# Norm outputs finished later: a two-block layer stack with hand-ordered vector work on one core

## The chip, the cores and the metric

One core of one Trainium2 chip runs the whole program. The metric is the device time of one execution in microseconds (us); smaller is better. The kernel before is given with three runs: 951.21, 951.55 and 951.58 us, median 951.55.

## What is computed

The input is 256 tokens of 1,024 channels. A first block (a mixer of three branches, then a gated feed-forward layer, both with RMS norms) is followed by two layers of a second block. The part of the second block that the change touches is, in the reference:

```python
for l in range(DEPTH_2):
    ...
    x = layer_norm(DEEPNORM_ALPHA * x + g1[:, None, :] * y, ln1_g[l], ln1_b[l])
    h = modulate(x, sh2, sc2)
    y = swiglu(h, ffn_w_gate[l], ffn_w_up[l], ffn_w_down[l])
    x = layer_norm(DEEPNORM_ALPHA * x + g2[:, None, :] * y, ln2_g[l], ln2_b[l])
```

`y` is a short convolution in layer 0 and forgetting attention (16 heads) in layer 1. `swiglu(h)` is `(silu(h @ w_gate) * (h @ w_up)) @ w_down` with 2,816 hidden channels. The six modulation vectors come from one vector `c`: `silu(c) @ w_ada + b_ada`.

## The kernel before

Activations lie with 128 channels on the partitions and the 256 tokens along the row, so a 1,024-channel activation is eight tiles (k = 0 to 7). Weights are float32 blocks of 128x128, read eight at a time (512 KB) by DMAs issued on SyncE. Each group of eight is split by ScalarE into a rounded high part `wh` (L145) and by VectorE into the rest `wl` (L151). Activations are split in the same way (`hilo`, L267 and L268). A product is three matmuls: `wh` by high, `wl` by high, `wh` by low. There are five buffers for split groups, and eight PSUM banks: four `acc`, two `lg`, two `ms`.

`single` and `pair` form one or two output columns over all k. `kouter` and `ksteps` take k in the outer loop for several columns, so that a product can begin when tile k = 0 is there. `gemv` forms one of 112 rows of the modulation vectors: a 512 KB DMA and one VectorE instruction (L372). How many of them go beside each unit of product is `grate`, set from the tuple `GR` as each stage begins; `fill` issues them. From any one constant or edit the order on an engine is found by a scheduler with a simulated timeline; `after(a, b)` adds an order to that (a behind b, no semaphore).

A norm ahead of a product is handled in two ways. After the first block's products (`post_rms`), the statistics are formed by matmuls against `rdim`, the reciprocal root by a chain of tiny VectorE instructions (`rsqrt`), and the result is spread by matmuls (`bcast`, L309). `warm` puts idle matmuls into the gaps. In the second block, three of the norms (`deep_norm` with `so`, then `ln_rows`) have a product that begins ahead of the norm: `lazy` multiplies six columns with the tiles that aren't normalised yet; `lazy_outs` then forms `out * R + nm * c0 + c1` from each of the six sums. `ln_next` meanwhile normalises and modulates the eight tiles for the remaining columns: per tile two VectorE instructions (L1071, L1072), two on ScalarE (L944, L267) and the low part on VectorE (L268). In a feed-forward layer the six outputs are three gate and up pairs, and `evac` applies silu, multiplies and splits them. In the attention layer they are six of the eight key tiles.

`unbroken(ins, free, act, head)` says which splits of later weights may go ahead of a norm's chain on VectorE: `free` of them ahead, the others behind the instructions `ins`; `head`, the chain's first instruction, goes behind those that are free. It also puts the next `gemv` behind the last of `ins`. `later` is a list of steps put off; `drain` issues one of them after each pair of columns.

In the attention loop TensorE's order is written by hand: the logits of head pair i, the transposes of pair i - 1, one k-step of the output projection's first four columns (`partial`), the values of pair i - 1.

Lines that the steps below speak of: `evac` L905, the loop over `first` L927, `deep_norm` L957, the freeing multiplication L1058, the addition L1066, the first norm's `rms_cols` L1102, the convolution's tiles L1189, the attention loop L1309 and the end of it L1322.

Of the kernel before, what the change touches and what calls it, by code (L numbers as in the profile page):

```python
# [17 lines left out]
P = 128  # L18
D = 1024
T = 256  # L20
# [9 lines left out]
GR = (0.75, 1.2, 0.375, 0.9, 1.05, 1.4, 0.25)  # L30
# [7 lines left out]
EXP_LN = 6  # L38
WARM = (3, 3, 5, 0)
# [26 lines left out]
class Net:  # L66
# [287 lines left out]
    def accum(self, acc, i, src, eps=0.0):  # L354

        if i == 0:
            self.nc.vector.tensor_scalar(acc, src, eps * NK, None, ALU.add)
        else:
            self.nc.vector.tensor_tensor(acc, acc, src, ALU.add)
# [539 lines left out]
    def ffn(self, l, X, R=None, first=(), rows=None):  # L899
# [3 lines left out]
        MH, ML = [], []  # L903

        def evac(g, u):  # L905
# [16 lines left out]
            MH.append(h)  # L922
            ML.append(lo)
# [33 lines left out]
    def deep_norm(self, wname, X, nk, gcol, ax, so=None, pre=()):  # L957
# [4 lines left out]
        zs, Z = [], ([], [])  # L962
# [5 lines left out]
        for c in range(NK):  # L968
# [11 lines left out]
            if so is not None:  # L980
# [4 lines left out]
                V.scalar_tensor_tensor(l, z, so[:, c, 0:1], h.bitcast(F32), op0=ALU.mult, op1=ALU.subtract)  # L985
# [65 lines left out]
    def lazy_outs(self, pss, R, nm, outs):  # L1051
# [3 lines left out]
        for ps, out in zip(pss, outs):  # L1055
            c = self.tmp("lz_c", (P, 2), bufs=4)
# [21 lines left out]
    def run(self):  # L1078
# [23 lines left out]
        rc = self.rms_cols()  # L1102
        rp = self.bcast(rc)
# [84 lines left out]
        for k in range(NK):  # L1188
            t = x1[k]  # L1189
            i0 = V.tensor_tensor(fg[k], fg[k], rp, ALU.mult)  # L1190
            i1 = V.tensor_tensor(t, t, fg[k], ALU.add)
            h, l = self.modulate(t, sc1[:, k:k + 1], sh1[:, k:k + 1])
# [4 lines left out]
        self.grate = GR[2]  # L1197
        self.pipeline(steps)
        self.unbroken([x[-1] for x in steps[1:]], 2, head=head)
# [57 lines left out]
        ks = []  # L1257
        for o in (0, 4):
            outs = [self.tmp("f_k", bufs=NK) for _ in first[o:o + 4]]
            self.lazy_outs(first[o:o + 4], *rows, outs)  # L1260
# [11 lines left out]
        for k in range(NK):  # L1272
# [5 lines left out]
            XQ[1].append(l)  # L1278
        self.inplace = True
# [25 lines left out]
        with self.tc.manual_schedule(engines={nc.tensor.engine}):  # L1305
# [16 lines left out]
            step(Y, NK - 1)  # L1322
        self.inplace = False
# [162 lines left out]
```

## Time and profile before

| | us |
|---|---|
| median of three runs | 951.55 |
| the profiled execution, its own time | 952.66 |
| its span in the trace | 950.8 |
| TensorE busy with matmuls | 916.2 |
| VectorE busy | 765.5 |
| ScalarE busy | 529.7 |
| SyncE's DMA queue, share of the 16 engines' span | 67.3% |

The profile was taken in one execution. Its span is what the trace covers, and 1.8 us of its time lie around it. An instruction's line is that of the kernel's code; `out<-in` are the program's tile names. Busy time of TensorE is modelled for the ends of matmuls, so it shows gaps in the stream, and not how fast the stream runs. A row's last bracket is the engine's idle time just before the instruction and what ended it.

### The profile page before, as it was taken

To read this page: it belongs to the slowest core of one execution; us is meant where nothing else is said; L and a number is where in the kernel's file an instruction comes from. 1 tells how busy PE (TensorE), PEld (TensorE's weight loads), DVE (VectorE), ACT (ScalarE), POOL (GpSimd) and SP (SyncE) were. 2 spreads that over 40 slices of the span, in tenths; PEclk is the share of its full clock that TensorE was granted. 3 is DMA by queue.
4 is the path that set the end of the run, shared out by engine and by line. 5 is a ranking of instruction groups with operands and counts; after the bars stand their busy time and mean duration, and the time that the engine had idled before them with its cause. 6 is when DMAs were issued, how large, how long until landed. Compare 5 with 4: busy or idle time off the path is not lost.

```text
span 950.8 us, 18969 instructions
## 1 busy us (share of the span) xinstructions
PE 916.2 (96%) x7434; PEld 884.6 (93%) x7434; DVE 765.5 (81%) x1463; ACT 529.7 (56%) x958; POOL 19.9 (2%) x66
## 2 busy tenths in 40 slices
PE   7999999999999899998999999999998999999995
PEld 7888899999999899998999999988887899999995
DVE  7897667999989789679899989898776897665554
ACT  7585755544444465557755454468665486544432
POOL 1111000000000000000000000000000000000001
PEclk9999999999999999999999999999999999999998
DMA  8774337899999787554899999845563458766631
GB/s 297 238 224 136 97 108 266 289 349 326 329 306 394 240 274 262 176 155 133 268 374 351 364 327 342 301 155 159 177 217 114 126 165 271 217 190 186 186 102 45
DMA packets 62345, 219.56 MB, mean 231 GB/s; under 512 B 7112, under 2 KB 8784, under 8 KB 62256
## 3 DMA queue, kind: packets, MB, share of 16 engines
q1 hardware_dynamic: 61056, 215.06, 67.3%
q0 software_dynamic: 1056, 3.16, 1.2%
q8 instruction: 58, 0.95, 0.4%
q14 instruction: 31, 0.25, 0.1%
q10 hardware_dynamic: 144, 0.13, 0.0%
HBM read 217.26 MB, written 2.63 MB: 231 GB/s over the span
## 4 chain that ended last, share of the span: by engine, by line
PE 84%; DVE 8%; ACT 3%; issue 2%; DMA 2%; SPq 0%; DVEq 0%; ACTq 0%
PE acc L165 19%; PE acc L163 19%; PE acc L164 19%; PE acc L198 4%; PE acc L199 4%; PE acc L204 4%; DVE wl L151 3%; PE lg L165 1%; PE lg L163 1%; PE lg L164 1%; DMA raw<-wts 1%; PE acc L254 1%; PE acc L252 1%; PE acc L253 1%; ACT wh L145 1%
## 5 line engine op out<-in xcount | busy, mean ns | idle before, releaser
L145 ACT ACTIVATE wh<-raw 128x1024 fp32r<-128x1024 f32 (+2 forms) x296 | 307.4, 1046 | 230.1 <-PE acc L165 112.4
L151 DVE TENSOR_TENSOR wl<-raw,wh 128x1024 fp32r<-128x1024 f32 (+2 forms) x296 | 355.1, 1208 | 82.8 <-ACT wh L145 80.9
L163 PE MATMUL acc<-yh,wh 128*128 128x256 f32 x544 | 152.3, 280 | 0.9 <-ACT yh L267 0.9
L165 PE MATMUL acc<-yl,wh 128*128 128x256 f32 x544 | 152.6, 281 | 0.5 <-DVE yl L268 0.5
L164 PE MATMUL acc<-yh,wl 128*128 128x256 f32 x544 | 151.9, 280 | 0.0
L163 PE MATMUL acc<-xh,wh 128*128 128x256 f32 x528 | 148.7, 282 | 0.0
L165 PE MATMUL acc<-xl,wh 128*128 128x256 f32 x528 | 148.3, 281 | 0.0
L164 PE MATMUL acc<-mh,wl 128*128 128x256 f32 x528 | 148.2, 281 | 0.0
L165 PE MATMUL acc<-ml,wh 128*128 128x256 f32 x528 | 148.1, 281 | 0.0
L163 PE MATMUL acc<-mh,wh 128*128 128x256 f32 x528 | 148.1, 281 | 0.0
L164 PE MATMUL acc<-xh,wl 128*128 128x256 f32 x528 | 148.0, 280 | 0.0
L372 DVE SCALAR_TENSOR_TENSOR gw<-gw,cact 128x1024 f32<-128x1024 f32 x112 | 135.2, 1220 | 0.6 <-DMA gw<-ada 0.5
L163 PEld LDWEIGHTS acc<-yh,wh 128*128 128x128 f32 x544 | 102.4, 188 | 1.1 <-ACT yh L267 1.1
L165 PEld LDWEIGHTS acc<-yl,wh 128*128 128x128 f32 x544 | 102.1, 188 | 0.8 <-DVE yl L268 0.7
L164 PEld LDWEIGHTS acc<-yh,wl 128*128 128x128 f32 x544 | 102.5, 188 | 0.0
L163 PEld LDWEIGHTS acc<-xh,wh 128*128 128x128 f32 x528 | 99.4, 188 | 1.4 <-issue 0.9
L164 PEld LDWEIGHTS acc<-xh,wl 128*128 128x128 f32 x528 | 99.5, 189 | 0.3
L165 PEld LDWEIGHTS acc<-ml,wh 128*128 128x128 f32 x528 | 99.5, 189 | 0.0
L163 PEld LDWEIGHTS acc<-mh,wh 128*128 128x128 f32 x528 | 99.5, 188 | 0.0
L165 PEld LDWEIGHTS acc<-xl,wh 128*128 128x128 f32 x528 | 99.3, 188 | 0.2 <-issue 0.2
L164 PEld LDWEIGHTS acc<-mh,wl 128*128 128x128 f32 x528 | 99.3, 188 | 0.0
L198 PE MATMUL acc<-xh,wh 128*128 128x256 f32 (+1 forms) x256 | 66.6, 290 | 9.7 <-ACT wh L145 5.5
(416 smaller groups left out, 1635.7 us busy)
## 6 DMA issues: line engine op xcount, KB each, us to landing
raw<-wts SPq DMA_DIRECT2D x288, 512.0 KB, 4.6
gw<-ada SPq DMA_DIRECT2D x112, 512.0 KB, 5.3
raw<-wts SPq DMA_DIRECT2D x6, 256.0 KB, 5.7
m_scr<-m_row POOLq DMA_DIRECT2D x2, 768.0 KB, 6.7
ax<-xT SPq DMA_DIRECT2D x4, 256.0 KB, 4.8
m_b<-m_scr POOLq DMA_DIRECT2D x8, 128.0 KB, 3.8
out<-fg SPq DMA_DIRECT2D x8, 128.0 KB, 1.8
cst<-cst SPq DMA_DIRECT2D x1, 588.5 KB, 6.7
```

The source lines that it names most:

```text
L145: i = self.aw = nc.scalar.activation(self.wh[:, d], r, AF.Copy)
L151: self.anchor = nc.vector.tensor_tensor(self.wl[:, d], r, self.wh[:, d].bitcast(F32), ALU.subtract)
L163: m = [mm(ps, wh, xh, start=start, stop=False), mm(ps, wl, xh, start=False, stop=False), mm(ps, wh, xl, start=False, stop=stop)]
L164: mm(ps, wl, xh, start=False, stop=False),
L165: mm(ps, wh, xl, start=False, stop=stop)]
L198: m.append(mm(outs[i], wh, X[0][k], start=k == 0 and i % per == 0, stop=False))
L199: m.append(mm(outs[i], wl, X[0][k], start=False, stop=False))
L204: m.append(mm(outs[i], wh, X[1][k], start=False, stop=False))
L252: mm(outs[tt], h, wh, start=k == 0 and (tt == 0 or not one), stop=False)
L253: mm(outs[tt], l, wh, start=False, stop=False)
L254: mm(outs[tt], h, wl, start=False, stop=k == NK - 1 and (tt == 1 or not one))
L372: i = nc.vector.scalar_tensor_tensor(t, t, 1.0, self.cact, op0=ALU.mult, op1=ALU.mult, accum_out=self.ada[:, g:g + 1])
```

## The change

The outputs formed ahead of a norm are now freed by their multiplication alone (L1058). The addition, the gate, the product and the split are returned as closures. In the two feed-forward layers they go to `later` (behind the eight residual steps that are there already), so one finished pair of hidden channels is issued beside each of three later pairs of columns; their sums lie in six tiles `fz` of the layer's pool. In the attention layer the six additions are issued after the query tiles. The small tile `lz_c` has six buffers for four.

Beside that: `GR[1]`, `GR[2]` and `GR[4]` move rows of the modulation vectors between stages. The first norm gets an `unbroken` with seven free splits. The convolution's tile k = 0 takes a shorter way from the norm to its high part, with the residual's own update for that tile at the end. After the attention loop the first later weight split goes behind the last softmax maximum, and all others go behind the last low part of the attention output. In the third such norm, the six accumulations of c = 4 to 6 go behind the last low part. The hidden tiles `mh`, `ml` are 256 wide instead of 258, and a pad of 192 bytes is set aside ahead of them by a `memset` on GpSimd.

```diff
-GR = (0.75, 1.2, 0.375, 0.9, 1.05, 1.4, 0.25)
+GR = (0.75, 0.85, 0.65, 0.9, 1.15, 1.4, 0.25)
+SHIFT = 192
+LATE = 3
+FREE0 = 7
...
+    def shift(self, pool, n):
+
+        self.nc.gpsimd.memset(self.tl(pool, [P, n // 4], "pad", bufs=1), 0.0)
...
-            h = self.tl(self.fp, [P, T + 2], "mh", F32R)[:, 0:T]
-            lo = self.tl(self.fp, [P, T + 2], "ml", F32R)[:, 0:T]
+            h = self.tl(self.fp, [P, T], "mh", F32R)
+            lo = self.tl(self.fp, [P, T], "ml", F32R)
...
-            outs = [self.tmp("ff_g" if q % 2 == 0 else "ff_u") for q in range(o, min(2 * n, o + 4))]
-            self.lazy_outs(first[o:o + 4], *rows, outs)
+            outs = [self.tl(self.fp, [P, T], "fz", bufs=6) for q in range(o, min(2 * n, o + 4))]
+            fins = self.lazy_outs(first[o:o + 4], *rows, outs)
             for j in range(0, len(outs), 2):
-                evac(*outs[j:j + 2])
+                self.later.append(lambda a=(len(MH), outs[j], outs[j + 1], fins[j:j + 2]): finish(*a))
+                MH.append(None)
+                ML.append(None)
...
             if so is not None:
+                if pre and c == NK - 1:
+                    for i in late:
+                        self.after(i, lz)
...
-                    self.accum(zacc, c, z)
-                    self.accum(sacc, c, sq)
+                    i = self.accum(zacc, c, z), self.accum(sacc, c, sq)
+                    if c > LATE:
+                        late += i
...
-        for c, out in zip(cs, outs):
+
+        def finish(c, out):
             w = self.tmp("md_h")
-            self.after(A.activation(w, nm, AF.Identity, scale=c[:, 0:1], bias=c[:, 1:2]), a)
-            self.after(V.tensor_tensor(out, out, w, ALU.add), i)
+            self.after(A.activation(w, nm, AF.Identity, scale=c[:, 0:1], bias=c[:, 1:2]), self.his[-1])
+            self.after(V.tensor_tensor(out, out, w, ALU.add), self.steps[-1][-1])
...
         rc = self.rms_cols()
+        self.unbroken([self.tail], FREE0, head=self.head)
...
+            if k == 0:
+                xs, fs = (self.tl(self.lp, [P, T], "ln_w", bufs=4) for _ in range(2))
+                A.activation(xs, t, AF.Identity, scale=sc1[:, 0:1], bias=sh1[:, 0:1])
+                A.activation(fs, fg[0], AF.Copy, scale=sc1[:, 0:1])
+                i0 = V.tensor_tensor(fs, fs, rp, ALU.mult)
+                i1 = V.tensor_tensor(fs, fs, xs, ALU.add)
+                h, l = self.hilo(fs, "x")
...
+        i = V.tensor_tensor(fg[0], fg[0], R, ALU.mult)
+        self.after(i, self.lo)
+        V.tensor_tensor(x1[0], x1[0], fg[0], ALU.add)
...
             step(Y, NK - 1)
+        self.unbroken([self.mxs, self.lo], 0)
```

## Rows read from the trace of the kernel before

**Rows 1.** Page, part 1: engine, busy us, share of the span, instructions.

```profile
PE 916.2 (96%) x7434; PEld 884.6 (93%) x7434; DVE 765.5 (81%) x1463; ACT 529.7 (56%) x958; POOL 19.9 (2%) x66
```

**Rows 2.** Windows by stage: length, busy us (count) per engine, granted clock, DMA.

```profile
314.00:330.00 16.00, 12.44 (x91) 11.25 (x91) 10.86 (x29) 6.64 (x11) 0.13 (x2) 1.00 0.62 199
436.00:452.00 16.00, 13.50 (x108) 12.69 (x107) 16.00 (x38) 14.84 (x31) 0.00 (x0) 1.00 0.44 133
628.00:642.00 14.00, 12.81 (x81) 10.89 (x80) 13.57 (x30) 12.40 (x25) 0.00 (x0) 1.00 0.54 184
642.00:666.00 24.00, 24.00 (x134) 19.86 (x134) 19.74 (x38) 19.13 (x40) 0.00 (x0) 1.00 0.53 158
717.00:732.00 15.00, 12.18 (x85) 10.03 (x84) 8.94 (x17) 6.76 (x17) 0.00 (x0) 0.89 0.55 176
732.00:750.00 18.00, 15.65 (x123) 14.70 (x121) 15.47 (x33) 9.88 (x19) 0.00 (x0) 1.00 0.41 118
```

**Rows 3.** Timeline of VectorE and TensorE, first norm: start, us, engine, instruction, idle.

```profile
28.50 1.23 DVE L151 TENSOR_TENSOR wl<-raw,wh 128x1024 fp32r<-128x1024 f32 x1 [0.85 <-ACT wh L145]
30.39 1.23 DVE L151 TENSOR_TENSOR wl<-raw,wh 128x1024 fp32r<-128x1024 f32 x1
32.22 0.68 PE L309 MATMUL ms<-ident,nw_y 128*128 128x128 f32 x4 [0.90 <-DVE nw_y L290]
```

**Rows 4.** Timeline around the norm ahead of the convolution, by engine.

```profile
314.73 12.39 SPq L369 DMA_DIRECT2D gw<-ada  x5
...
320.96 1.22 DVE L372 SCALAR_TENSOR_TENSOR gw<-gw,cact 128x1024 f32<-128x1024 f32 x1
323.72 1.22 DVE L372 SCALAR_TENSOR_TENSOR gw<-gw,cact 128x1024 f32<-128x1024 f32 x1
...
325.32 0.60 ACT L944 ACTIVATE ln_w<-ax,adac,adac 128x256 f32<-128x256 f32 x1 [2.84 <-DVE ax L1191]
...
326.42 0.39 PE L198 MATMUL acc<-xh,wh 128*128 128x256 f32 x1 [1.77 <-ACT xh L267]
```

**Rows 5.** TensorE's waits, 436 to 452: total us, times, longest; one freeing multiplication.

```profile
PE acc L199 <- DVE wl L151: 2.0, 3, 0.9
PE acc L198 <- DVE ff_g L1058: 0.5, 1, 0.5
...
436.43 0.42 DVE L1058 TENSOR_TENSOR ff_g<-acc,zacc 128x256 f32<-128x256 f32 x1
```

**Rows 6.** Timeline at the key tiles: two additions, and TensorE's wait.

```profile
629.99 0.76 DVE L1066 TENSOR_TENSOR f_k<-f_k,md_h 128x256 f32<-128x256 f32 x2
...
635.07 0.72 PE L254 MATMUL acc<-wl,yh 128*128 128x512 f32 x2 [1.19 <-DVE wl L151]
```

**Rows 7.** Timeline, end of attention and third such norm; the last row a window.

```profile
716.65 4.63 DVE L151 TENSOR_TENSOR wl<-raw,wh 128x1024 fp32r<-128x1024 f32 x4
...
721.52 0.75 DVE L792 TENSOR_REDUCE a_mx<-lg 128x1 f32<-128x256 f32 x2
...
731.49 0.42 DVE L268 TENSOR_TENSOR yl<-ms,yh 128x256 fp32r<-128x256 f32 x1 [4.83 <-ACT yh L267]
...
748.02 0.42 DVE L978 TENSOR_TENSOR p_sq<-fg 128x256 f32<-128x256 f32 x1
...
744.97 0.39 PE L198 MATMUL acc<-xh,wh 128*128 128x258 f32 x1 [2.24 <-DVE fg L971]
...
726.80:730.20 3.40, 3.40 (x18) 0.52 0.34 133
```

**Rows 8.** Timeline of TensorE, the third norm's first remaining column.

```profile
766.75 0.39 PE L198 MATMUL acc<-yh,wh 128*128 128x256 f32 x1 [1.26 <-DVE ff_u L1058]
```

**Rows 9.** Windows of TensorE alone: gate columns (x tiles), then down-projection (mh, ml).

```profile
180.00:250.00 70.00, 70.00 (x598) 1.00 0.93 331
...
556.00:606.00 50.00, 50.00 (x424) 1.00 0.95 333
```

More of the change, by code (lines that the diff above doesn't have):

```diff
@@ L356, in accum @@
         if i == 0:
-            self.nc.vector.tensor_scalar(acc, src, eps * NK, None, ALU.add)
-        else:
-            self.nc.vector.tensor_tensor(acc, acc, src, ALU.add)
+            return self.nc.vector.tensor_scalar(acc, src, eps * NK, None, ALU.add)
+        return self.nc.vector.tensor_tensor(acc, acc, src, ALU.add)
     def gemv(self, n=1):
@@ L903, in ffn, with evac @@
         MH, ML = [], []
-        def evac(g, u):
+        self.shift(self.fp, SHIFT)
+        def evac(g, u, j=None):
             if R is not None:
@@ L917, in evac, with finish @@
                 V.tensor_tensor(m, s, u, ALU.mult)
-            h = self.tl(self.fp, [P, T + 2], "mh", F32R)[:, 0:T]
-            lo = self.tl(self.fp, [P, T + 2], "ml", F32R)[:, 0:T]
+            h = self.tl(self.fp, [P, T], "mh", F32R)
+            lo = self.tl(self.fp, [P, T], "ml", F32R)
             nc.scalar.activation(h, m, AF.Copy)
             self.gbound = V.tensor_tensor(lo, m, h.bitcast(F32), ALU.subtract)
-            MH.append(h)
-            ML.append(lo)
+            if j is None:
+                MH.append(h)
+                ML.append(lo)
+            else:
+                MH[j], ML[j] = h, lo
+        def finish(j, g, u, fins):
+            for f in fins:
+                f()
+            evac(g, u, j)
         wg, wu = f"g{l}", f"u{l}"
@@ L961, in deep_norm @@
         V = nc.vector
-        zs, Z = [], ([], [])
+        zs, Z, late = [], ([], []), []
         if so is None:
@@ L984, in deep_norm @@
                 nc.scalar.activation(h, z, AF.Copy, scale=so[:, c, 0:1])
-                V.scalar_tensor_tensor(l, z, so[:, c, 0:1], h.bitcast(F32), op0=ALU.mult, op1=ALU.subtract)
+                lz = V.scalar_tensor_tensor(l, z, so[:, c, 0:1], h.bitcast(F32), op0=ALU.mult, op1=ALU.subtract)
                 Z[0].append(hf)
@@ L1055, in lazy_outs @@
         for ps, out in zip(pss, outs):
-            c = self.tmp("lz_c", (P, 2), bufs=4)
+            c = self.tmp("lz_c", (P, 2), bufs=6)
             a = A.activation(c, ps[:, T:], AF.Copy)
@@ L1062, in lazy_outs @@
             cs.append(c)
-        for c, out in zip(cs, outs):
+        def finish(c, out):
             w = self.tmp("md_h")
-            self.after(A.activation(w, nm, AF.Identity, scale=c[:, 0:1], bias=c[:, 1:2]), a)
-            self.after(V.tensor_tensor(out, out, w, ALU.add), i)
+            self.after(A.activation(w, nm, AF.Identity, scale=c[:, 0:1], bias=c[:, 1:2]), self.his[-1])
+            self.after(V.tensor_tensor(out, out, w, ALU.add), self.steps[-1][-1])
+        return [lambda c=c, out=out: finish(c, out) for c, out in zip(cs, outs)]
     def ln_mod(self, z, rows, s1, b1, tag="y", pool=None):
@@ L1189, in run @@
             t = x1[k]
-            i0 = V.tensor_tensor(fg[k], fg[k], rp, ALU.mult)
-            i1 = V.tensor_tensor(t, t, fg[k], ALU.add)
-            h, l = self.modulate(t, sc1[:, k:k + 1], sh1[:, k:k + 1])
+            if k == 0:
[5 more added lines that the diff above has]
+                h, l = self.hilo(fs, "x")
+            else:
+                i0 = V.tensor_tensor(fg[k], fg[k], rp, ALU.mult)
+                i1 = V.tensor_tensor(t, t, fg[k], ALU.add)
+                h, l = self.modulate(t, sc1[:, k:k + 1], sh1[:, k:k + 1])
             steps.append([i0, i1, self.lo])
@@ L1197, in run @@
         self.grate = GR[2]
+        R = self.tl(self.lp, [P, T], "rp", bufs=1)
+        A.activation(R, rp, AF.Copy)
         self.pipeline(steps)
+        i = V.tensor_tensor(fg[0], fg[0], R, ALU.mult)
+        self.after(i, self.lo)
+        V.tensor_tensor(x1[0], x1[0], fg[0], ALU.add)
         self.unbroken([x[-1] for x in steps[1:]], 2, head=head)
@@ L1256, in run @@
         x, XK, rows = self.ln_next(zs, rows, so, (g, b), (0, 4, 1, 3, 5, 7))
-        ks = []
+        ks, fins = [], []
         for o in (0, 4):
             outs = [self.tmp("f_k", bufs=NK) for _ in first[o:o + 4]]
-            self.lazy_outs(first[o:o + 4], *rows, outs)
+            fins += self.lazy_outs(first[o:o + 4], *rows, outs)
             ks += outs
@@ L1278, in run @@
             XQ[1].append(l)
+        for f in fins:
+            f()
         self.inplace = True
```

## The prediction, made before the change was run

> **What bounds the kernel now.** I read the busy times first. TensorE is busy for 916.2 of 950.8 us, VectorE for 765.5 [rows 1]. So TensorE leaves 34.6 us idle in all, and a change that adds no matmul can only win from that, from matmuls that follow each other faster, and from stretches at a lower clock. The windows by stage say where the idle time is: 3.56 us ahead of the convolution, 2.50 in the first norm with outputs formed ahead, 1.19 at the key tiles, 2.82 and 2.35 at the end of attention [rows 2]. In the window of 2.50 VectorE has no idle time at all (16.00 of 16.00), at the key tiles 13.57 of 14, after attention 15.47 of 18: there VectorE's order decides when TensorE goes on. The rows that end TensorE's waits [rows 3 to 8] then tell which VectorE or ScalarE step came last at each place.
>
> **The change part by part.** Times before and after are those of the profiled execution.
>
> *The first norm.* The reciprocal root's chain is interrupted by a weight split at 30.39, whose work takes 1.14 us before the next instruction starts, and TensorE waits 0.90 for the chain's end [rows 3]. The new call lets seven groups ahead of the chain's head. Counted by issue, four groups belong to the first product, so groups 4 to 10 are free; the split at 28.50 is group 10, and the one at 30.39 is group 11, the first that is bound behind the chain's end. So nothing new comes ahead of the head, and the interruption goes. What is late next is TensorE itself: its products last until 31.3. I take -0.9; the bounds are -1.1 (the whole split) and 0, if ScalarE's next split still stands ahead of the copies that free PSUM.
>
> *Ahead of the convolution.* Two rows of the modulation vectors stand inside the norm's chain, at 320.96 and 323.72, each holding VectorE for 1.15 us; then the modulation of tile 0 takes 0.60 on ScalarE, and the first product starts at 326.42 [rows 4]. The rows are late because five of their DMAs sat in SyncE's queue for 12.39 us [rows 4]. With `GR[1]` at 0.85 the down-projection issues 6 x 2.75 x 0.85 = 14 rows for 19.8 before. The five that lag are within the 5.8 taken away; weight DMAs behind them on SyncE move up as well. They come back in the convolution (10.4 rows for 6), where TensorE shows no idle. The shorter way of tile 0 removes the 0.60: its two ScalarE steps need nothing of the norm, and its update, two VectorE steps of 0.4, goes behind the last low part. Sum: -1.15 - 1.15 - 0.6 = -2.9. The idle matmuls after the spread end near 323.5, so no more is to be had: -3.4 at best. If one gate row stays in the chain it is -1.7, with both -0.6.
>
> *The first feed-forward layer's norm.* TensorE waits three times, 2.0 us together, for a weight split on a VectorE that is never idle, and 0.5 for the freeing multiplication [rows 2, 5]. Put off are six additions, three products and three splits: two additions take 0.76 [rows 6], so twelve such steps are about 4.6 us of VectorE, and as many ScalarE steps. That is more than the 2.0, so those waits go; the 0.5 stays, since the multiplications keep their place. I take -2.0, bounds -0.5 and -2.5. Put off, they stand beside three later pairs, four VectorE steps or 1.5 us in each pair. There VectorE is the cover, with the five split buffers between it and TensorE; if a pair's splits came late by that, it would cost up to 1.5 us for each of three pairs in both layers.
>
> *The key tiles.* TensorE waits 1.19 for a split; two additions, 0.76, stand ahead of it on VectorE [rows 6]. They go, and the six additions with their six ScalarE steps (0.6 each, as the modulation [rows 4]) move to 642 to 666. ScalarE is busy for 19.13 of 24 there [rows 2], so 3.6 us more leaves it about 1 us free, and behind it are the copies of the value tiles and the splits. I take -0.7, between -1.2 and +1.5.
>
> *The end of attention.* Four splits, 4.63 us from 716.65, stand ahead of the last pair's maxima, which start at 721.52 although the first split alone would be over at 717.8; the last low part of the output comes at 731.49, and TensorE meanwhile runs 3.4 us at a granted clock of 0.52, the lower level of 1.2 GHz, after gaps [rows 7]. The new call puts the second split behind those maxima and three behind the last low part. So the softmax starts three splits or 3.4 us earlier, and without the half clock (18 matmuls in 3.4 us, where the full clock needs half of it) the low part comes about 5 us earlier. Against that, three splits, 3.4 us, move into the stretch from 731.49 to 748.44, which ends with VectorE's last square ahead of the statistics [rows 7] and is nearly all VectorE [rows 2]. The late accumulations change their order, not their sum, and let go the 2.24 that TensorE waited for the last output's PSUM [rows 7]. If VectorE stays the bound the gain is 5 - 3.4 = 1.6; if the splits fall into its gaps, all 5. I take -3.0, nearer to the first; bounds -5.4 (all idle time of the two windows) and +3.4 (the softmax isn't earlier).
>
> *The third such norm.* TensorE waits 1.26, for a freeing multiplication [rows 8], which keeps its place: 0, bounds -1.3 and +0.5.
>
> *The gate rows of the second down-projection*, 1.15 for 1.05, make 19.0 of 17.3. No row shows one in a chain there; a late one costs 1.15 as in the first [rows 4]. I take 0, bounds 0 and +1.2.
>
> *Addresses.* Matmuls on the hidden tiles follow each other every 50 / 424 = 117.9 ns, those on the normalised tiles every 70 / 598 = 117.1 [rows 9], all at the full clock. The new widths and the pad move only the former, 1,584 of them (22 x 8 x 3, three layers): 1.3 us if they reach the others' pace. No row shows the new addresses, so half of it, -0.7, with -2.6 and +1.3 as ends. The Trainium skill, "SBUF — State Buffer", section "Who interferes with whom", says that TensorE's reads never wait on anyone; by that both kinds would run alike and this term would be 0. The trace differs by 0.8 ns a matmul at an equal clock, so I keep the term.
>
> The `memset` on GpSimd and the wider `lz_c` cost nothing: GpSimd is busy for 19.9 us in all [rows 1] and has nothing queued that TensorE waits for.
>
> Sum: -0.9 - 2.9 - 2.0 - 0.7 - 3.0 - 0.7 = -10.2. The profiled execution takes 952.7, so 942.5; the median shown is 1.1 lower, so **941.4**.
>
> **The rivals.** *The late splits give back the end of attention*: VectorE bounds 731 to 748 and takes three more splits while the softmax is ordered as before. +3.4 for -3.0 gives 947.8. For it speaks 15.47 of 18 [rows 2], against it that the maxima have nothing else to wait for from 717.8.
>
> *The orders don't come out as the edits say.* The scheduler may set gate rows into the chain again and other splits ahead of the maxima; then only the feed-forward waits go and other places lose as much: 950 to 953. For it: the gaps [rows 4] are orders that it chose while the chain was ready. Against it: three of the edits are fixed orders.
>
> *TensorE starves behind the last low part, and its clock falls* (slower). The splits of columns 5 to 7 are now all issued after that point. If VectorE first does the four ready columns (four sums, four low parts, four accumulations, 12 x 0.4 = 4.8 us), TensorE idles, and the 72 matmuls of three columns run at the lower clock, as the 18 did [rows 7]: 72 x 0.09 = 6.5 us. With 3.4 for the splits and the 4.8 of waiting that is +14.7, and the other terms give back 7.2: 959. It decides from where the first of the three splits starts over some 2 us behind the last low part. The Trainium skill, "TensorE: Matmul & The Clock Gate", section "What's actually happening", says that the default state is throttled and that activity releases the throttle; the trace agrees, 0.52 just after gaps [rows 7]. Against this rival: the splits are ready at once, the sums only after the last k-step.
>
> **How the numbers follow.** The forecast, gains of 5 to 15 us, has 0.66; the late splits that give back 0.14; the orders that don't come out 0.11; the starved TensorE 0.09. About 0.2% is what a measurement of this kernel can tell from no change: 1.9 us, so 949.65 and 953.45 are the borders. Faster: 0.66 + 0.14 + 0.03 of the third = 0.83; same 0.08; slower 0.09. The bounds of the six terms don't all meet at one end; the lower end is 936.0 (end of attention and addresses at their best), the upper 949.5, which takes in the second case and the near edge of the third.
>
> **What would show it.** Right: no gate row between the root's first step and the first product ahead of the convolution; no wait for L151 in the first feed-forward norm, with additions beside pairs of columns 9 to 11 after it; maxima of the last pair within 1 us of 717.8 less what was won before; the full clock there; the statistics matmul of the third norm 3 us earlier relative to those maxima's logits. Wrong: a wait for L151 in the four output columns after attention, a gate row in the norm behind the second down-projection, ScalarE without idle time at the value tiles, and matmuls on hidden tiles at 118 ns as before.

## The result, and the profile after

The changed kernel takes 945.69 us (median of four runs, 945.10 to 947.32) beside 951.54 for the kernel before on the same chip: a ratio of 0.9942, 95% interval 0.9930 to 0.9954. That is a gain of 5.9 us, on the forecast side and inside the range, and 4.3 us short of the forecast 941.4.

The page's busy row, and some of the largest of TensorE's waits in after (total us, times, longest), answer to [rows 1] and to the waits in [rows 3 to 8]:

```profile
PE 914.4 (97%) x7434; PEld 883.6 (93%) x7434; DVE 764.2 (81%) x1465; ACT 530.1 (56%) x960; POOL 20.1 (2%) x69
...
PE acc L201 <- DVE fg L988: 2.1, 1, 2.1
...
PE ms L1039 <- DVE za L365: 1.9, 1, 1.9
PE acc L202 <- DVE wl L154: 1.7, 2, 0.9
PE acc L201 <- DVE fz L1079: 1.7, 2, 1.3
PE ms L825 <- ACT a_pt L814: 1.2, 1, 1.2
```

Line numbers have moved: a split is L154 for L151, the freeing multiplication L1079 for L1058, the outputs' multiplication L988 for L971, the sums ahead of a norm stay in `accum` (L365), their statistics are L1039 for L1018. Of the waits for splits one in the first feed-forward norm is left (0.9). The wait for L988 is as long as before, 2.1 beside 2.24 [rows 7], and one for the late sums (L365) is new.

To see where time went, take the start of the same matmul in each trace and subtract: from the first matmul of a norm's statistics to the first product behind it, and so on. The stages below are such differences, in us. Between after and its second profile they differ by 0.02 or less, attention by 0.17. "Low part" stands for the first matmul of the output projection's last k-step, which follows it; attention counts from the last transpose of its first head pair; the third norm ends with the first matmul on its normalised tiles; "half clock" is where the granted clock falls to its lower level for 3.4 us (the last ten us of the span are left out). The norm between the convolution and the second layer, 13.84 or 13.85 in every kernel, isn't listed.

| stage | before | after | after again | freed only | no end order | old tiles | rows and first | lazy 42 |
|---|---|---|---|---|---|---|---|---|
| first feed-forward layer | 189.01 | 188.54 | 188.55 | 189.07 | 188.55 | 189.08 | 188.56 | 188.55 |
| norm ahead of the convolution | 7.08 | 4.39 | 4.39 | 7.08 | 4.39 | 4.39 | 6.55 | 4.39 |
| convolution to statistics | 96.63 | 97.43 | 97.43 | 98.10 | 97.43 | 97.43 | 98.67 | 97.43 |
| second such layer, to its statistics | 172.88 | 170.75 | 170.73 | 171.16 | 170.73 | 171.16 | 170.62 | 170.73 |
| its norm, keys, values, to the first attended pair | 63.92 | 63.88 | 63.86 | 63.28 | 63.86 | 63.88 | 63.27 | 63.87 |
| attention to the last low part | 57.82 | 54.38 | 54.55 | 56.48 | 58.59 | 54.11 | 53.69 | 54.17 |
| to the third norm's statistics | 16.73 | 18.82 | 18.83 | 16.74 | 16.34 | 18.82 | 18.82 | 19.72 |
| third norm | 15.49 | 17.10 | 17.09 | 15.50 | 15.50 | 15.50 | 15.50 | 14.07 |
| third such layer | 173.55 | 172.86 | 172.87 | 173.29 | 172.87 | 173.29 | 172.86 | 172.53 |
| half clock at | 726.7 | 743.0 | 743.4 | 328.0, 724.0 | 722.3 | 737.1 | 740.0 | 736.9 |

The other columns are experiments below. Read before against after: the norm ahead of the convolution wins 2.7 and the convolution gives back 0.8; the two later feed-forward layers win 2.1 and 0.7, the first 0.5; the key tiles nothing; attention's end 3.4, of which 2.1 come back ahead of the statistics and 1.6 more in the norm.

Ahead of the convolution, VectorE's timeline of after (start, us, instruction, idle) has the root's last step, then tile 0's two short steps, and no `gw` between, where [rows 4] had two; TensorE's first product:

```profile
320.39 0.16 DVE L297 SCALAR_TENSOR_TENSOR nw_y<-nw_q,nw_y 128x2 f32<-128x2 f32 x1
321.51 0.42 DVE L1219 TENSOR_TENSOR ln_w<-ln_w,ms 128x256 f32<-128x256 f32 x1 [0.96 <-PE ms L316]
321.97 0.43 DVE L1220 TENSOR_TENSOR ln_w<-ln_w,ln_w 128x256 f32<-128x256 f32 x1
...
322.91 0.39 PE L201 MATMUL acc<-xh,wh 128*128 128x256 f32 x1 [0.23 <-ACT xh L274]
```

At the end of attention, VectorE's timeline of after: one split and then the last pair's maxima, a second split, the last low part; three splits at once behind it; splits and sums until the statistics can start.

```profile
713.04 1.22 DVE L154 TENSOR_TENSOR wl<-raw,wh 128x1024 fp32r<-128x1024 f32 x1
714.17 0.75 DVE L798 TENSOR_REDUCE a_mx<-lg 128x1 f32<-128x256 f32 x2
...
715.94 1.22 DVE L154 TENSOR_TENSOR wl<-raw,wh 128x1024 fp32r<-128x1024 f32 x1
...
723.17 0.42 DVE L275 TENSOR_TENSOR yl<-ms,yh 128x256 fp32r<-128x256 f32 x1 [3.49 <-ACT yh L274]
723.51 3.49 DVE L154 TENSOR_TENSOR wl<-raw,wh 128x1024 fp32r<-128x1024 f32 x3
726.91 2.04 DVE L988 SCALAR_TENSOR_TENSOR fg<-acc,adac,fg 128x256 f32<-128x256 f32 x5
...
738.64 0.87 DVE L1002 SCALAR_TENSOR_TENSOR xl<-fg,lns,xh 128x256 fp32r<-128x256 f32 x2
739.44 0.41 DVE L365 TENSOR_TENSOR za<-za,p_sq 128x256 f32<-128x256 f32 x1
...
742.01 1.10 PE L1039 MATMUL ms<-za,odim 128*128 128x512 f32 x2 [1.88 <-DVE za L365]
```

The order is the one that the edits ask for, and the low part is 8.3 us earlier than at 731.49 [rows 7], 4.9 of which were won before attention. Then VectorE is never idle until the statistics.

### The profile page after: what moved, and what is told of

Same layout as the page of the kernel before. It is cut to its first block, busy times and chain, and to the rows that moved or that the text cites. A ratio compares the mean times of both kernels' runs of the same rounds, so it can differ in the third digit from the quotient of the medians.

```text
span 945.5 us, 18974 instructions
## 1 busy us (share of the span) xinstructions
PE 914.4 (97%) x7434; PEld 883.6 (93%) x7434; DVE 764.2 (81%) x1465; ACT 530.1 (56%) x960; POOL 20.1 (2%) x69
## 4 chain that ended last, share of the span: by engine, by line
PE 86%; DVE 7%; ACT 3%; DMA 2%; issue 1%; SPq 0%; DVEq 0%; ACTq 0%
PE acc L166 19%; PE acc L168 19%; PE acc L167 19%; PE acc L201 5%; PE acc L202 5%; PE acc L207 4%; DVE wl L154 2%; DMA raw<-wts 2%; PE lg L168 1%; PE lg L166 1%; PE lg L167 1%; ACT wh L148 1%; PE acc L257 1%; PE acc L255 1%; PE acc L256 1%
## 5 line engine op out<-in xcount | busy, mean ns | idle before, releaser
L154 DVE TENSOR_TENSOR wl<-raw,wh 128x1024 fp32r<-128x1024 f32 (+2 forms) x296 | 354.7, 1206 | 75.3 <-ACT wh L148 73.7
```

The costliest lines, as they stand in the source:

```text
L154: self.anchor = nc.vector.tensor_tensor(self.wl[:, d], r, self.wh[:, d].bitcast(F32), ALU.subtract)
```

## The experiments

Medians of five to ten executions, with the ratio to the kernel before on the same chip and its 95% interval; the kernel after, run once more, stands among them:

| run | median, us (lowest to highest) | ratio to before |
|---|---|---|
| after again | 946.12 (945.25 to 947.72) | 0.9942 (0.9929 to 0.9955) |
| freed only | 949.49 (947.51 to 950.18) | 0.9971 (0.9961 to 0.9980) |
| no end order | 947.49 (947.17 to 949.22) | 0.9956 (0.9941 to 0.9970) |
| all behind the maxima | 945.98 (944.49 to 947.11) | 0.9934 (0.9919 to 0.9949) |
| no late sums | 946.81 (945.37 to 947.48) | 0.9942 (0.9928 to 0.9956) |
| both | 946.32 (945.37 to 946.96) | 0.9941 (0.9929 to 0.9954) |
| old tiles | 948.70 (946.55 to 949.12) | 0.9963 (0.9949 to 0.9977) |
| tile 0 the long way | 946.84 (945.73 to 948.41) | 0.9947 (0.9934 to 0.9959) |
| rows and first | 948.28 (947.32 to 948.78) | 0.9966 (0.9953 to 0.9978) |
| keys at once | 945.38 (944.99 to 947.42) | 0.9942 (0.9929 to 0.9955) |
| four extra matmuls | 946.32 (945.13 to 947.53) | 0.9948 (0.9935 to 0.9960) |
| lazy 42 | 944.33 (943.76 to 944.55) | 0.9925 (0.9912 to 0.9939) |

Most intervals overlap, so the times alone separate few of these; the stages do.

### Freed chains alone

The kernel before with the new `lazy_outs`, its `finish` and the freed `first` columns, and nothing else:

```
-        for c, out in zip(cs, outs):
+        def finish(c, out):
...
+                self.later.append(lambda a=(len(MH), outs[j], outs[j + 1], fins[j:j + 2]): finish(*a))
...
+        for f in fins:
+            f()
```

> The kernel before with one part of the change alone: of the outputs formed ahead of a norm only the multiplication is done at once; sums, gates and splits stand beside later columns. All other parts are left as before. My theory puts the gain of this part at 2.7 us (first feed-forward norm 2.0, key tiles 0.7), so 948.8. The trace of the kernel after reads lower: about 1.3 at the feed-forward norm and nothing at the key tiles, so 950.2. Rival: this part carries the change, 946 to 947. Rival on the other side: the late VectorE steps delay later splits, 951.5 or more.

Measured 949.49, a gain of 2.3 us by the medians (951.81 for before), between the two numbers of the theory. By the stages the second layer wins 1.72, the third 0.26, the key tiles 0.64, together 2.6. Its profile also had a second stretch at half clock in the convolution (328.0), which is why that stage reads 98.10: against before its matmuls fall 1.5 behind from 328.9 to 332.0 and stay there. Attention was 1.3 shorter too (56.48 for 57.82), for which no run gives the cause. TensorE's waits at the same two places, the first norm's window and then the key tiles', against 2.0 and 1.19 in [rows 5, 6]:

```profile
PE acc L199 <- DVE wl L151: 0.9, 1, 0.9
PE acc L198 <- DVE fz L1068: 0.5, 1, 0.5
...
PE acc L254 <- DVE wl L151: 0.7, 1, 0.7
```

So the change's namesake is worth 2.6 us alone. Of after's 5.9 it is 2.0 (1.72 + 0.26), since the key tiles win nothing there, as the next run shows.

### Keys at once

```
             ks += outs
+        for f in fins:
+            f()
...
-        for f in fins:
-            f()
         self.inplace = True
```

> The kernel after with the sums of the six key columns done at once again, as before; the feed-forward columns stay freed. Theory: freeing the key tiles moved the wait and did not shorten the stage (63.9 us from the second feed-forward norm to the first attention gap both before and after), so 945.7 to 946.3, with one wait of about 1.2 us at the key tiles' second product for the two of 0.8 and 1.0 in after. Rival: the part is worth the forecast 0.7, then 946.7. Rival on the other side: the later sums load ScalarE at the value tiles and cause the wait of 0.9 to 1.5 at 669, so without them 945.0.

945.38, and the stage is 63.88, as in after. The one wait of 1.2 that the theory expected did not come back; the waits at the key tiles are those of after to the tenth:

```profile
PE acc L257 <- DVE wl L154: 0.6, 1, 0.6
PE acc L255 <- ACT wh L148: 0.5, 1, 0.5
```

With the gate rows' new pace the freed key tiles are worth nothing. With the old pace they are worth 0.64 (freed only 63.28, and 63.27 in the run "rows and first" below). The second wait, for a split's high part on ScalarE, stands in the traces with the new pace alone.

### Gate rows and the first norm

```
-GR = (0.75, 0.85, 0.65, 0.9, 1.15, 1.4, 0.25)
+GR = (0.75, 1.2, 0.375, 0.9, 1.05, 1.4, 0.25)
...
-        self.unbroken([self.tail], FREE0, head=self.head)
```

> The kernel after with two parts undone that lie in different stages: the order at the first norm (first 75 us) and the pace of the gate rows in the down-projections and the convolution. Read stage by stage. Theory for the rows: two of them stand in the norm ahead of the convolution again, 2 x 1.15, so the convolution starts 2.1 to 2.3 us later against the norm's first matmul; and the wait of 0.8 us inside the convolution (359.8 in after) goes, since it comes from the rows moved there. Rival: that wait has nothing to do with the rows and stays. Theory for the first norm: 0.3 to 0.4 us, what after showed there, not the forecast 0.9. Together 947.8 to 948.4 where after has 946.0; rival on the other side: the scheduler sets other work in the norm and nothing comes back, 946.

948.28, 2.2 over after again. The norm takes 6.55 for 4.39, and VectorE's timeline shows a gate row inside the root's chain and one between tile 0's two steps:

```profile
320.32 0.22 DVE L296 SCALAR_TENSOR_TENSOR nw_q<-nw_y,nw_v 128x1 f32<-128x1 f32 x1
320.46 1.22 DVE L378 SCALAR_TENSOR_TENSOR gw<-gw,cact 128x1024 f32<-128x1024 f32 x1
...
322.98 0.42 DVE L1218 TENSOR_TENSOR ln_w<-ln_w,ms 128x256 f32<-128x256 f32 x1 [0.96 <-ACT wh L148]
323.32 1.22 DVE L378 SCALAR_TENSOR_TENSOR gw<-gw,cact 128x1024 f32<-128x1024 f32 x1
```

So the rows are worth 2.16 there. The other half of the theory failed: the wait in the convolution did not go but grew, from 0.5 to 1.8 (TensorE for `c_c`, L1249 in after). In after it is this row:

```profile
360.58 0.39 PE L166 MATMUL acc<-xh,wh 128*128 128x256 f32 x1 [0.53 <-ACT c_c L1249]
```

At the first norm, 0.4: from the 81st matmul (some 17.5 us) to the norm ahead of the first feed-forward layer the run takes 108.63, after 108.20. Of the profiles with the new order ten have 108.20 to 108.34, and "no late sums", whose 81st matmul came half a microsecond earlier, 108.73; without it before has 108.89 and "freed only" 108.62. So this part is known to some 0.3 only.

### Tile 0 the long way

```
-            if k == 0:
+            if k < 0:
```

and the update of tile 0 behind the last low part goes.

> The kernel after with tile 0 ahead of the convolution formed as before: update first, then its modulation on ScalarE, then the high part. Theory: its 0.6 us on ScalarE come back ahead of the convolution's first product, and 0.4 of one VectorE step with it, 946.3 to 946.7. Rival: the two gate rows were the whole gain there, TensorE's start hangs on the broadcast alone, 945.7. Rival on the other side: the short way adds two VectorE steps to the convolution's start and a ScalarE copy, and they cause the wait of 0.5 to 0.8 at 359.8, so without them 945.2.

946.84. The norm takes 4.97 instead of 4.39, so tile 0's short way is worth 0.58, the theory's 0.6 without its 0.4 for a VectorE step. The convolution is 97.43 as in after, so the short way does not cause its wait. Old rows with the long way (before) have 96.63, new rows with either way 97.43, old rows with the short way 98.67: neither edit alone explains it.

### Old tiles

```
-            h = self.tl(self.fp, [P, T], "mh", F32R)
+            h = self.tl(self.fp, [P, T + 2], "mh", F32R)[:, 0:T]
...
-        self.shift(self.fp, SHIFT)
```

> The kernel after with the hidden tiles as before: two columns wider, no pad ahead of them. Theory: matmuls on them follow each other at 117.9 ns again (424 in the 50 us from 262 to 312) instead of 117.1 (427), 1,584 of them, so 1.3 us over after, 947.0. Rival: the closer matmuls are due to something else, and all stays as in after, 945.7. Rival on the other side: the pad costs more than it gives, 945 or less.

948.70, 2.6 over after again by the medians, with 0.0014 on either side of the ratio. The stages give the part more sharply: 0.53, 0.43 and 0.42 in the three layers, 1.4 in all. Windows of TensorE alone in the first down-projection (length, busy us and count, clock, DMA), of after and then of this run:

```profile
262.00:312.00 50.00, 50.00 (x427) 1.00 0.96 355
```

```profile
262.00:312.00 50.00, 50.00 (x424) 1.00 0.95 350
```

427 for 424 [rows 9] is 117.1 ns for 117.9. The width and the pad went back together, so which of them it was is not shown. The run gave something else: it has after's code at the end of attention, but its half clock began at 737.1 and not at 743.0, and its third norm takes 15.50 for 17.10.

### The end of attention

Four kernels. Without the new order of splits:

```
-        self.unbroken([self.mxs, self.lo], 0)
```

> The kernel after without the line that holds the weight splits behind the last pair's maxima and the last low part of attention; all else as after (945.7). Theory: what the earlier softmax wins (3.4 us of splits, some half clock) the three late splits give back on a VectorE that never idles behind the last low part; so the time stays within 0.7 of after, 945.0 to 946.4, the last low part comes some 3 to 5 us later and the third norm's statistics follow it some 3 to 5 us sooner. Rival: the line is worth the forecast 3.0, then 948.7. Rival on the other side: the line costs, because it moves the splits to the busiest stretch, then 944 or less.

With all later splits behind the maxima alone:

```
-        self.unbroken([self.mxs, self.lo], 0)
+        self.unbroken([self.mxs], 0)
```

> The kernel after, but all later splits are bound behind the last pair's maxima alone, none behind the last low part. Theory: the maxima stay where they are in after (714.2), the splits fall into VectorE's waiting time between the maxima and the last low part, at most 1 to 2 us of them delay it, and the stretch behind it loses 3.4 us of VectorE work; the sum is a gain of 1 to 2 us over after, 943.7 to 944.7. Rival: VectorE has no free time there, so each split delays the low part by as much as it relieves later, 945.7. Rival on the other side: the low part is late by all three splits and the clock falls as before, 947 or more.

With the sums as before:

```
-LATE = 3
+LATE = 7
```

> The kernel after with the late sums undone: the accumulations of columns 4 to 6 ahead of the third norm are no longer put behind the last column's low part. Theory: the same VectorE work in another order, 945.2 to 946.2; TensorE's wait of 1.9 us for the sum at the statistics goes and comes back as a wait for the outputs' multiplications. Rival: the late sums cost what the statistics wait for them, so without them 943.8. Rival on the other side: they win the 2.2 us that TensorE waited for the last output's place in PSUM, so without them 947.5 or more.

And the last two edits together:

> The kernel after with two of its orders loosened: the later splits are bound behind the last pair's maxima alone (e3), and the sums ahead of the third norm are not put late (e5). From the first attention gap to the end of the third norm after took 91.8 us, e3 90.4, e5 90.1. Theory: the two waits are different ones, so both gains add, 88.7 in that region and 942.6 for the whole. Rival: VectorE bounds the region, and each of the two only uses the same idle time, so 90 and 944.0. Rival on the other side: with neither order the scheduler sets splits and sums as in the kernel before, 91.5 and 945.5 or more.

> The kernel after once more, unchanged, on the chip of the runs beside it, so that they are compared with it and not only with the kernel before: 945.7 us, within 1.0. Its profile should show the shape of the first one: last pair's maxima about 714, last low part about 723, statistics of the third norm about 742. Rival: the profiled run of after was an outlier in places (it was the longest of its four), and the region from the first output of attention to the third norm is shorter than the 91.8 us that it showed by over 1 us.

Three stages in a row, and their sum (the expectations count from the last gap ahead to the wait behind the norm's first column, 1.5 us more). The beginning of attention varies for other reasons: from its start to the last pair's logits "freed only", which has before's order at the end, takes 41.13 and before 42.12. So "from the logits" gives the same sum counted from the first matmul of those logits:

| | to the low part | to the statistics | third norm | sum | from the logits | half clock at |
|---|---|---|---|---|---|---|
| before | 57.82 | 16.73 | 15.49 | 90.04 | 47.92 | 726.7 |
| after | 54.38 | 18.82 | 17.10 | 90.30 | 47.80 | 743.0 |
| after again | 54.55 | 18.83 | 17.09 | 90.47 | 47.96 | 743.4 |
| old tiles | 54.11 | 18.82 | 15.50 | 88.43 | 46.20 | 737.1 |
| no end order | 58.59 | 16.34 | 15.50 | 90.43 | 48.08 | 722.3 |
| all behind the maxima | 55.91 | 17.62 | 15.42 | 88.95 | 47.11 | 738.2 |
| no late sums | 54.27 | 18.82 | 15.49 | 88.58 | 46.37 | 736.8 |
| both | 57.72 | 16.74 | 15.50 | 89.96 | 47.78 | 722.2 |

These logits in before and in after:

```profile
715.82 0.92 PE L772 MATMUL lg<-f_k,a_q 64*128 64x256 f32 x8
```

```profile
711.31 1.19 PE L778 MATMUL lg<-f_k,a_q 64*128 64x256 f32 x8
```

The order of splits brings the low part 4 us forward (58.59 to 54.55) and puts 2.5 on the way from there to the statistics (16.34 to 18.83). "No end order", at 947.49, lies between its theory (up to 946.4) and its rival (948.7); by its profile it is even with after, and 1.7 to 1.9 longer from the logits than "old tiles" and "no late sums", which have after's order of splits and a half clock that keeps out of the norm. The late sums change nothing, 18.82 with and without, since without the edit the sums stand behind the last output's multiplication all the same (from 737.62, for 736.09). With the splits behind the maxima alone three of them stand in a row between the maxima and the reciprocal, so VectorE has no free time there: the reciprocal starts 5.2 us behind the maxima, for 2.9 in after. Counted from the logits the low part is 2.2 later (14.07 for 11.87). The way from it to VectorE's last sum is 2.5 shorter (16.21 for 18.68), but the statistics start only 1.2 sooner: TensorE, at half clock from 738.2, reaches them 1.4 behind that sum, for 0.15 in after. The clock apart, each split delays the low part by about what it relieves later, which is the rival. Its timeline of VectorE, with TensorE's statistics:

```profile
713.53 0.74 DVE L798 TENSOR_REDUCE a_mx<-lg 128x1 f32<-128x256 f32 x2
...
715.30 3.48 DVE L154 TENSOR_TENSOR wl<-raw,wh 128x1024 fp32r<-128x1024 f32 x3
718.70 0.17 DVE L800 RECIPROCAL a_sm<-a_sm 128x4 f32<-128x4 f32 x1
...
740.39 0.41 DVE L365 TENSOR_TENSOR za<-za,p_sq 128x256 f32<-128x256 f32 x1
...
742.21 1.02 PE L1039 MATMUL ms<-za,odim 128*128 128x512 f32 x2
```

"Both" has the same order up to the low part (its reciprocal 5.2 behind the maxima too) and the same waits of TensorE, but a half clock that began at 722.2, ahead of the low part. The same stretch in "all behind the maxima" and then in "both" (TensorE alone):

```profile
722.20:725.60 3.40, 2.92 (x26) 1.00 0.61 241
```

```profile
722.20:725.60 3.40, 3.40 (x19) 0.50 0.67 259
```

Its low part is 1.5 later against the logits (15.54 for 14.07): that is what the half clock costs there. Its statistics start 0.15 behind the last sum again. By the times neither of the two reached its theory (945.98 for 943.7 to 944.7, 946.32 for 942.6), and "no late sums" is 0.6 above the upper end of its own (946.81 for 946.2).

After again repeats after in every stage, the long norm too, so that was no outlier. The gain of 1 to 2 us that "all behind the maxima" and "no late sums" seem to show against after is the norm's 1.6, and "old tiles" has it too, with none of their edits.

What decides the 1.6 is where the half clock falls. In the six kernels of this table whose half clock begins between 722 and 739 the third norm takes 15.4 to 15.5; in both profiles of after, and in that of "tile 0 the long way" (743.6, 17.14), it falls on the statistics and the first products behind them. Counted from the logits the order is worth 1.5 to 1.7 against before in "old tiles" and "no late sums", and nothing in after. Before's own half clock lies ahead of its low part (726.7), and the one of "no end order" too, where it cost 1.5 in "both". If it costs as much in them, an estimate that no run checks, the order of the splits by itself is worth next to nothing, and the gain is that the half clock falls where VectorE is the bound. Windows of the same place in after again, and in "old tiles" (busy us and count of TensorE, its loads, VectorE, ScalarE, GpSimd; clock, DMA):

```profile
724.00:742.00 18.00, 14.28 (x116) 13.64 (x115) 18.00 (x35) 9.82 (x19) 0.00 (x0) 1.00 0.64 205
742.00:747.00 5.00, 4.59 (x16) 3.78 (x17) 1.58 (x5) 1.75 (x4) 0.00 (x0) 0.66 0.01 2
```

```profile
724.00:742.00 18.00, 15.69 (x117) 15.06 (x115) 18.00 (x36) 9.81 (x19) 0.00 (x0) 0.91 0.65 204
742.00:747.00 5.00, 4.52 (x29) 3.97 (x30) 2.36 (x8) 2.52 (x4) 0.00 (x0) 1.00 0.01 4
```

Ahead of the statistics VectorE is busy for 18.00 of 18 in both, so a slower TensorE costs nothing there; behind them TensorE does 16 matmuls for 29. The profiled execution is the longest of its group in after (947.32 of 945.10 to 947.32), after again (947.72) and "tile 0 the long way" (948.41), and the shortest in "old tiles" (946.55) and "no late sums" (945.37). That fits executions of one kernel that differ by where the half clock falls, but only the profiled ones show it, and in "four extra matmuls", where it falls well, the profiled execution (946.69) is the fourth of five.

### Filling TensorE's wait

Four matmuls whose result is overwritten, ahead of the statistics:

```
+        if self.nlazy == 2:
+            self.dummy = [mm(st[:, 0, :], self.ident, z, start=True, stop=True) for _ in range(4)]
         mm(st, self.odim, both, start=True, stop=False)
...
+        if self.nlazy == 2:
+            self.after(self.dummy[0], ms[LZ[2] - 1])
```

> The kernel after with four more matmuls whose result is overwritten: they stand on TensorE between the 30th product formed ahead and the third norm's statistics, where it waits 2.2 us for a sum (4 x 0.43 = 1.7 us). Theory: the 3.4 us at half clock fall into the norm because TensorE idles just ahead of it; in the norm they cost 1.6 us (18.6 from the statistics to the norm's end where they fall there, 17.0 where not). With TensorE busy the norm takes 17.0 in the profiled run, and the time is 944.5 to 945.5. Rival: the idle time before 737 is enough, the clock falls in the norm all the same, and the extra matmuls delay nothing: 946.1. Rival on the other side: the extra matmuls end behind the sum and delay the statistics, 946.5 to 947.5.

946.32. The half clock fell ahead of the statistics (738.2) and the norm takes 15.43, as the theory has it; but at that clock the products and the extra matmuls end late, and the statistics start 1.2 us later (20.04 for 18.82), the rival on the other side. In "all behind the maxima" the half clock began at 738.2 as well, and without extra matmuls they started 1.4 behind the last sum (1.4 here too), so how much of the 1.2 the extra matmuls cost by themselves is not shown. Extra matmuls and statistics:

```profile
741.03 2.17 PE L1040 MATMUL ms<-fg,ident 128*128 128x256 f32 x8
743.04 1.02 PE L1041 MATMUL ms<-za,odim 128*128 128x512 f32 x2
```

The same place filled with products that are needed anyway:

```
-LZ = (18, 27, 30)
+LZ = (18, 27, 42)
```

> The kernel after with 42 instead of 30 of the third norm's products ahead of its statistics: 12 matmuls of 0.117 us, 1.4 us of work that must be done anyway, moved into TensorE's wait for the sum. Theory: as with the extra matmuls the half clock keeps out of the norm, 17.0 from the statistics to its end; the work moved leaves a longer wait (1.5 + 1.4) for the freed columns at the norm's end, so the time is no better than there, 944.5 to 945.7. Rival: the idle time only changes its place, and the clock falls behind the longer wait, 946 or more.

944.33, and all five executions (943.76 to 944.55) are below the fastest of after's nine in its two groups of runs (945.10) and of "keys at once" on the same chip (944.99): the best kernel here, below both of the given ones, 0.0017 under after by the ratio, though the intervals overlap. The profile's sum of the two stages is 33.79 (19.72 + 14.07), 0.5 less than after's without the half clock (34.3) and 2.1 less than with it; the third layer takes 0.33 less. So 0.8 of the gain over after is the moved work; that the rest is the half clock's place is likely, but the executions without a profile don't show it. TensorE's waits from 720 to 765 no longer hold one for the sum, nor for a freeing multiplication, but one for a split:

```profile
PE acc L201 <- DVE fg L988: 2.1, 1, 2.1
PE acc L202 <- DVE wl L154: 0.8, 1, 0.8
PE acc L201 <- ACT yh L274: 0.5, 1, 0.5
```

The longer wait that the expectation feared at the norm's end did not come: with the later products done, the freeing multiplications came in another order, and the wait of 1.3 in front of them became one of 0.8 for a split.

## Why the prediction was right, and where it was not

The sign and the range held: 945.69 lies between 936.0 and 949.5. The forecast gain of 10.2 came out as 5.9, near the lower edge of the 5 to 15 that had most of the chances. Two bounds were off: the idle time of the two windows [rows 2] is 5.2 and not 5.4, and with both terms at their best the lower end is 937.1 and not 936.0. By the steps of the sum:

- **First norm**, -0.9: measured -0.4. The split did leave the root's chain, as said. It now stands right behind it, at 31.03, and the next thing that VectorE does for TensorE, the copy `m_T`, comes at 32.66; TensorE is idle for 0.51 there.
- **Ahead of the convolution**, -2.9: measured -2.69, made of 2.16 for the rows and 0.58 for tile 0, for 2.3 and 0.6. The step that failed is the cover: "They come back in the convolution (10.4 rows for 6), where TensorE shows no idle". From 340 to 372 VectorE is busy for 29.72 us instead of 28.67, TensorE waits, and 0.8 comes back. What exactly holds the column's place in PSUM is not settled; rows and short way act together.
- **First feed-forward norm**, -2.0: measured -1.72 alone, and 0.26 more in the third layer, for which the prediction took 0. This is the best of the terms: two of three waits for a split are gone and the 0.5 for the freeing multiplication stays, as written.
- **Key tiles**, -0.7: 0 in after, though -0.64 without the new pace of the gate rows. The term was right for the edit alone and wrong beside another edit, which the prediction added up as if they were independent.
- **End of attention**, -3.0: measured -1.3 with the half clock ahead of the statistics (54.38 + 18.82 + 15.50 for 90.04), and +0.3 with it behind (90.30). Counted from the logits it is -1.7 (47.92 to 46.20) and nothing, and by the estimate above nearly all of the -1.7 is the half clock. This is the largest miss. The prediction worked out 5 - 3.4 = 1.6 for the case that VectorE stays the bound, had the row for that case (15.47 of 18, [rows 2]), and still took a value halfway to "all 5". VectorE was the bound: its way from the low part to the last sum took 18.68 for 16.58. The late sums, which were to let go of the 2.24 us for the last output's place, let go of nothing, because the sums in question stood behind that multiplication without the edit too. And the half clock did not vanish: in after it moved to where it costs, the first rival's mechanism with part of the third's.
- **Third norm**, 0: nothing seen, the clock apart; the wait of 1.26 is 1.3 now.
- **Gate rows of the second down-projection**, 0: with the key tiles freed in both, the stage behind it takes 63.88 with the new pace and 63.28 with the old. This is the 0.6 that the key tiles lost. One row more than before stands between that norm's statistics and its chain (at 608.21), which the prediction named as a sign of being wrong.
- **Addresses**, -0.7: measured -1.4 (0.53 + 0.43 + 0.42). The hidden tiles reached the others' pace in full; only the half that was taken off for doubt was wrong. The rule of the Trainium skill that the prediction weighed against this term ("SBUF — State Buffer", section "Who interferes with whom") is about engines that make one another wait. It gave no reason to put the term at 0: the same instructions at the same clock differ by 0.8 ns with the width and place of the tiles, and that does not contradict it.

The measured parts add to -0.4 - 2.7 + 0.8 - 1.7 - 0.3 - 1.3 - 1.4 = -7.0 where the half clock stays out of the norm, and -5.4 where it falls in it; the profiled executions differ by 5.3 (952.66 and 947.32), the medians, of executions that may be of both kinds, by 5.9. So 3.2 of the 4.3 us that the forecast had too much are steps: 1.7 at the end of attention, 0.8 the convolution, 0.7 the key tiles, 0.5 the first norm, 0.5 in the two best terms, less 1.0 that the addresses and the third layer gave beyond it. The other 1.1 lies within what the clock takes. That the number fell well inside the range is partly luck: steps that were 4.2 too high met 1.0 of gain that was not counted on, and the range was 13.5 wide.

Of the signs that the prediction named, the gate rows ahead of the convolution and the pace on the hidden tiles came as written. One wait for a split is left in the first feed-forward norm. The third norm's statistics came 1.7 us earlier against the last pair's logits (30.69 for 32.43), not 3.

The second rival, orders that don't come out, is ruled out by the timelines above. The third (a TensorE that starves behind the low part) did not happen: TensorE's stream has no gap over 0.4 us from the low part at 723.2 to 734.5.

## What to carry to other kernels

Before you credit an order that frees one stage, look where the displaced work lands, and where the lower clock falls: if the engine is busy for the whole of the next window, most of its length comes back (2.1 to 2.5 of 3.4 us here), and where a gain was put between two ends, the bounded end is what came out here. Edits that share an engine are priced together, since a gain of 0.6 can vanish by another edit's pace. A wait of TensorE that can't be shortened is a place for work that must be done anyway; twelve products moved there gave 0.8 by the stages, more than any other order of the splits and sums that was tried in place of after's.

## What the runs showed of the hardware

- Every profile here has one stretch of 3.4 us at the lower clock between 722 and 747, where TensorE has several gaps. Its place differs between kernels with the same order of work there (737.1 in "old tiles", 743.0 in after), so the work there does not settle it alone. Its cost was 1.5 us ahead of the low part ("both" beside "all behind the maxima"), nothing where VectorE was the bound ("old tiles"), and 1.6 us in the norm (after).
- In the profiles here, most stages' lengths between two matmuls repeat to 0.02 us where nothing touches them, while whole executions of one kernel differ by up to 4.6 us (949.38 to 954.00, the kernel before). Parts of 0.3 us can be read by stages that the times can't tell.
- Matmuls of 128x256 on the hidden tiles go from 117.9 to 117.1 ns when only the tiles' width and a pad ahead of them change, 1.4 us over three layers.
